# Blocks of 16 for the triangular inverse, and low weight parts kept in DRAM

## The chip, the cores and the metric

The kernel runs on one core of one Trainium2 chip. The metric is the device time in microseconds of one launch. One core has five engines that run their own instruction streams in order: TensorE (PE, with its weight loads shown as PEld), VectorE (DVE), ScalarE (ACT), GpSimd (POOL) and SyncE (SP). In this kernel every DMA is issued from SP's queue.

## The reference

One layer of a hybrid recurrent trunk: a norm, one wide projection, four recurrent mixers over four heads of 64 each, gates, an output projection and a final norm. 1024 prompt tokens are one sequence; 8 further rows are single steps of 8 sequences with carried states.

```python
h = rms_norm(x, norm_g)
proj = jnp.matmul(h, w_in)            # split among the four mixers and their gates
# gated delta rule (GDN), chunks of 64 tokens:
low  = jnp.where(strict, einsum('nbhid,nbhjd->nbhij', kb, k) * decay, 0.0)
sol  = triangular_solve(low + eye, [vb, kb * exp(gc)], lower=True, unit_diagonal=True)
# RWKV-7: s = s*exp(w) - (s @ kk) (kk*a)^T + v k^T, one token after the other
mixed = concatenate([o_gla, o_s5, o_gdn, o_rwkv])
x = x + mixed @ w_out;  y = rms_norm(x, final_g)
```

Both the delta rule and RWKV-7 are computed here in chunks of 64 tokens, and each chunk of each head needs the inverse of a unit triangular 64x64 matrix.

## The kernel before, in words

The tokens are worked through in two halves of 512 (the second one carries the 8 further rows too, so 520 columns). In each half the four mixers work on two pairs of heads each.

**Streams.** A projection of 128 output columns is `stream` (L270): its 1024x128 weights come in two chunks of 256 KB, and each chunk goes through `wsplit` (L261). SP loads it raw (`wr`, 3 buffers, L263), ACT rounds it to the high part (`wh`, 2 buffers, L266), and POOL subtracts that from the raw one for the low part (`wl`, 2 buffers, L267). PE then does three matmuls for each block of 128 rows: high weights by high inputs, high by low, low by high (L278). There are 30 projections and 8 output streams in a half, so 38 streams and 76 chunks; both halves load and split the same weights. The streams of `w_out` come last in each half (`out_stream`, L1273); those of the second half end the kernel (`tail`).

**Inverses.** `inverse` (L288) is called by each unit of RWKV and GDN: 2 mixers x 2 pairs x 2 halves = 8 times, for 16 matrices of 64x64 each. The diagonal blocks of 32x32 are gathered through DRAM so that each of 128 partitions holds one block row set (L298 writes `d1`, L301 reads it back as `LT`). VectorE eliminates them in 31 steps of two instructions: a product into `DP` (L308) and a sum into `DT` (L310). The result goes out to DRAM (`d2`, L313) and comes back into `XT` (L315). VectorE transposes (L319), and two rounds of small matmuls on PE (L324, L327), each with an ACT copy behind it, join the blocks of 32 to 64. The chunk recurrence of the unit reads `XT`.

**Order.** A unit is a generator in four stages: its projections, its preparation (stage 1, which ends with the matrix `Gt` or `Gg`), the inverse (stage 2), the recurrence (stage 3). `ORDER` (L33) lists the tokens that advance the units; R, D, L, S, g, W stand for RWKV, GDN, GLA, S5, a gate and the weights of S5, an accent for the second half. `PRI` (L32) brings a stage forward by so many instructions; R2 and D2 are the inverses. From these a scheduler fixes the order of instructions on each engine at build time, so a change in lengths moves instructions everywhere. `late` holds an instruction behind another one without a semaphore.

## Time and profile before

| | us |
|---|---|
| runs | 1046.91, 1058.57, 1059.12 (median 1058.57) |
| profiled execution | 1059.9 |
| its span, first to last instruction | 1058.1 |

| engine | busy us | share | instructions |
|---|---|---|---|
| PE | 929.8 | 88% | 5994 |
| PEld | 764.5 | 72% | 5994 |
| DVE | 698.9 | 66% | 1843 |
| ACT | 462.4 | 44% | 1088 |
| POOL | 391.1 | 37% | 439 |

The mean granted clock of TensorE is 0.854 of full. Busy time of PE is a union of modelled durations that overlap, so two matmuls that start 0.12 us apart and last 0.28 us each count as one stretch; a PE that is busy may still be far from its rate. A float32 matmul shows as two records, so 16 of them in the program are 32 in a count. The first half's own work lies in the span from about 0 to 440 us, the second half's from about 440 on, with the first half's output streams moved in between its recurrences.

### The profile page before, as it was taken

The page shows a single profiled execution, that of the slowest core. Times are in us where ns is not written, and L with a number is a line of the kernel's source. Part 1 is how long each engine was busy: PE and PEld are TensorE (multiplying, and loading weights), DVE is VectorE, ACT ScalarE, POOL GpSimd, SP SyncE. Part 2 cuts the span into 40 slices and gives each one's busy share as a digit, 9 for nine tenths or more (in the row PEclk, how much of TensorE's full clock was granted, in tenths as well). Part 3 has the DMA queues.
Part 4 walks back from the last instruction along what each step waited for, and adds up shares of the span by engine and source line. Part 5 has one row for each costly group of instructions (what it writes and reads, how often), then busy time and mean ns, then how long its engine had stood idle before and what let it go on. Part 6 is the DMA issues. An engine that isn't in the chain of part 4 may idle for free. (4 is left out here: it accounts for less than half of the span.)

```text
span 1058.1 us, 17042 instructions
## 1 busy us (share of the span) xinstructions
PE 929.8 (88%) x5994; PEld 764.5 (72%) x5994; DVE 698.9 (66%) x1843; ACT 462.4 (44%) x1088; POOL 391.1 (37%) x439
## 2 busy tenths in 40 slices
PE   3898989899998898797999989898998989897595
PEld 2676757678777686687788868777886968685594
DVE  8627895767548645836577979888976555725523
ACT  4355625331643423531663544554343354257233
POOL 2698654530221540015344513205523711432132
PEclk9999989975886866598999989868986969899697
DMA  7142423220220203125123332313121244437322
GB/s 234 56 143 77 137 74 81 80 60 5 77 63 28 81 29 120 58 64 160 50 81 96 100 91 80 92 27 85 33 62 40 83 132 132 147 117 240 139 80 91
DMA packets 85109, 95.91 MB, mean 91 GB/s; under 512 B 41640, under 2 KB 52016, under 8 KB 85024
## 3 DMA queue, kind: packets, MB, share of 16 engines
q1 hardware_dynamic: 85024, 94.83, 29.4%
q8 instruction: 47, 0.77, 0.3%
q14 instruction: 38, 0.31, 0.1%
HBM read 75.95 MB, written 16.72 MB: 88 GB/s over the span
## 5 line engine op out<-in xcount | busy, mean ns | idle before, releaser
L267 POOL TENSOR_TENSOR wl<-wr,wh 128x512 fp32r<-128x512 f32 x152 | 207.4, 1366 | 430.8 <-ACT wh L266 376.4
L278 PE MATMUL psp<-xhi,wh 128*128 128x260 f32 (+2 forms) x728 | 263.1, 362 | 4.8 <-DVE rx L357 2.2
L278 PE MATMUL psp<-xhi,wl 128*128 128x260 f32 (+2 forms) x728 | 254.0, 352 | 7.1 <-POOL wl L267 6.9
L278 PE MATMUL psp<-xlo,wh 128*128 128x260 f32 (+2 forms) x728 | 252.7, 348 | 0.7 <-DVE xlo L258 0.7
L278 PEld LDWEIGHTS psp<-xhi,wh 128*128 128x128 f32 x728 | 152.5, 209 | 26.4 <-issue 7.0
L278 PEld LDWEIGHTS psp<-xhi,wl 128*128 128x128 f32 x728 | 150.9, 208 | 26.3 <-POOL wl L267 10.9
L278 PEld LDWEIGHTS psp<-xlo,wh 128*128 128x128 f32 x728 | 152.6, 210 | 16.6 <-issue 4.4
L266 ACT CAST wh<-wr 128x512 fp32r<-128x512 f32 x152 | 93.6, 617 | 142.0 <-PE psp L278 73.5
L308 DVE TENSOR_TENSOR DP<-DT,LT 128x60 f32<-128x60 f32 (+24 forms) x248 | 76.2, 307 | 11.5 <-DMA LT<-d 5.5
L310 DVE TENSOR_TENSOR DT<-DT,DP 128x60 f32<-128x60 f32 (+24 forms) x248 | 77.0, 311 | 6.2
L278 PE MATMUL psp<-olo,wh 128*128 128x260 f32 (+1 forms) x192 | 64.5, 336 | 5.1 <-DVE olo L117 4.8
L278 PE MATMUL psp<-ohi,wh 128*128 128x260 f32 (+1 forms) x192 | 65.8, 345 | 3.4 <-ACT wh L266 1.9
L278 PE MATMUL psp<-ohi,wl 128*128 128x260 f32 (+1 forms) x192 | 63.8, 339 | 0.1
L278 PEld LDWEIGHTS psp<-olo,wh 128*128 128x128 f32 x192 | 38.3, 199 | 8.8 <-DVE olo L117 5.5
L278 PEld LDWEIGHTS psp<-ohi,wh 128*128 128x128 f32 x192 | 38.2, 200 | 6.9 <-ACT wh L266 2.3
L113 ACT ACTIVATE eg<-eg 128x260 f32<-128x260 f32 (+1 forms) x72 | 33.8, 485 | 18.7 <-DVE eg L200 18.2
L485 PE MATMUL psc<-UV,Gt 64*128 64x64 f32 (+1 forms) x256 | 39.8, 292 | 2.1 <-ACT UV L478 2.1
L278 PEld LDWEIGHTS psp<-ohi,wl 128*128 128x128 f32 x192 | 37.6, 198 | 3.0 <-POOL wl L267 0.4
L485 PEld LDWEIGHTS psc<-UV,Gt 64*128 64x128 f32 (+1 forms) x256 | 30.3, 189 | 11.5 <-issue 2.9
L117 POOL TENSOR_TENSOR df<-cum 128x256 f32<-128x256 f32 x48 | 30.4, 654 | 19.7 <-DVE cum L739 12.5
L764 PE MATMUL psb<-W 64*128 64x64 f32 x256 | 34.8, 319 | 0.1
L256 PE MATMUL psb<-constA,xn 128*128 128x128 f32 (+1 forms) x72 | 15.8, 375 | 20.3 <-DVE xn L252 9.9
(432 smaller groups left out, 1875.0 us busy)
## 6 DMA issues: line engine op xcount, KB each, us to landing
wr<-in_wct SPq DMA_DIRECT2D x120, 256.0 KB
wr<-in_wo SPq DMA_DIRECT2D x32, 256.0 KB
xn<-in_x SPq DMA_DIRECT2D x8, 512.0 KB
LT<-d SPq DMA_DIRECT2D x32, 128.0 KB
dgp<-gp SPq DMA_DIRECT2D x8, 256.0 KB
Gml<-dG SPq DMA_DIRECT2D x4, 512.0 KB
csT<-dph SPq DMA_DIRECT2D x4, 512.0 KB
dTl<-dT SPq DMA_DIRECT2D x4, 512.0 KB
```

Source lines behind the costliest of these rows:

```text
L113: A.activation(out, in_, func, bias=bias, scale=scale, **kw)
L117: return (G if ENG[name] == "G" else V).tensor_tensor(out, a, b, op)
L256: PE.transpose(pt[:, k, :n], xn[:n, (4 * b + k) * 128:(4 * b + k + 1) * 128], ident[:n, :n])
L266: A.copy(hi, raw)
L267: G.tensor_tensor(lo, raw, hi, ALU.subtract)
L278: X["mm"] = PE.matmul(p[:, :m], w[:, k % 4, :], x[:, k, c0:c0 + m], start=(i == 0 and s == 0), stop=(i == 7 and s == 2))
L308: V.tensor_tensor(tp[:, :m, :w], DT[:, :m, j:j + 1].to_broadcast([128, m, w]), LT[:, j:j + 1, j + 1:32].to_broadcast([128, m, w]), ALU.mult)
L310: V.tensor_tensor(DT[:, :m, j + 1:32], DT[:, :m, j + 1:32], tp[:, :m, :w], ALU.add)
L485: PE.matmul(o, l, r, start=start, stop=True, skip_group_check=True)
L764: PE.matmul(pg[:, c, :], W[HS[e], t], W[HS[e], t].rearrange("p (b f s) -> p f b s", f=2, s=s)[:, 1], start=True, stop=True)
```

## The change

The inverse works on diagonal blocks of 16, so VectorE has 15 steps of two instructions (30, not 62), on tiles half as wide. The gather through DRAM has one DMA for each block of 16 (twice as many), the read back two DMAs for four, the way out two for four, the way into `XT` eight for four. A round is added that joins 16 to 32: four more transposes on VectorE, 32 matmuls of 32x16, an ACT copy into `P16` (which takes the one buffer of `DP`), 32 matmuls of 16x16, four ACT copies. The two old rounds alternate between the pairs now. The zeros in `XT` are written whole by one POOL instruction.

The low part of a weight chunk is computed once: in the first half SP writes it to DRAM behind POOL's subtraction, in the second half SP loads it instead. 76 subtractions of POOL are gone, 76 stores and 76 loads of 256 KB are added, all in SP's queue. `ORDER` and `PRI` are other ones.

```diff
-PRI = {"R2": 4000, "D2": 2000, "R3": 4000, "D3": 2000, "L1": 1600, "R1": 600, "L0": 100, "L2": 600, "D0": 300, "D1": 1000}
+PRI = {"R2": 1875, "D2": 1000, "R3": 4000, "D3": 2000, "L1": 1600, "R1": 600, "L0": 100, "L2": 600, "D0": 150, "D1": 1250}
-ORDER = ("x W W t W W m R0 g6 R0 D0 W W M D0 D1 R1 W R0 R1 L0 R1 R0 L0 R1 D1 L0 g0 D0 D0 S g0 L1 g4 g6 D1 g3 g7 L1 D1 g2 L1 x' "
...
+ORDER = ("x W W t R0 m D0 W W g6 R0 W W W M D0 D1 R1 R0 R1 L0 R1 R0 L0 R1 D1 L0 g0 S g0 L1 D0 D0 g4 g6 D1 g3 g7 g2 L1 L1 D1 x' "
...
     def wsplit(src, key):
...
         A.copy(hi, raw)
-        G.tensor_tensor(lo, raw, hi, ALU.subtract)
+        if key in kept:
+            SP.dma_start(out=lo.bitcast(F32), in_=kept[key])
+        else:
+            G.tensor_tensor(lo, raw, hi, ALU.subtract)
+            kept[key] = drp.tile([128, 4, 128], F32, name=f"wk{len(kept)}")
+            SP.dma_start(out=kept[key], in_=lo.bitcast(F32))
...
     def inverse(Ga, XT, after):
...
+            for u in range(2):
+                r = slice(32 * f + 16 * u, 32 * f + 16 * u + 16)
+                for b, g in enumerate(Ga[p]):
+                    SP.dma_start(out=d1[p, f, u, nb * b:nb * b + nb].rearrange("(c e) s t -> s c e t", e=2), in_=g[r, :, :, r])
...
-        for j in range(31):
-            m = j // 4 + 1
-            w = 31 - j
+        for j in range(15):
+            m = j // 2 + 1
+            w = 15 - j
...
             V.tensor_tensor(tp[:, :m, :w], DT[:, :m, j:j + 1].to_broadcast([128, m, w]),
-                            LT[:, j:j + 1, j + 1:32].to_broadcast([128, m, w]), ALU.mult)
-            V.tensor_tensor(DT[:, :m, j + 1:32], DT[:, :m, j + 1:32], tp[:, :m, :w], ALU.add)
+                            LT[:, j:j + 1, j + 1:16].to_broadcast([128, m, w]), ALU.mult)
+            V.tensor_tensor(DT[:, :m, j + 1:16], DT[:, :m, j + 1:16], tp[:, :m, :w], ALU.add)
...
+        P16 = tmp.tile([128, 8, 16], F32, tag="DP", bufs=NB["DP"], name="P16")
+        for p, f in Q:
+            V.transpose(D16[at(p, f)], XT[at(p, f), :, 32 * f:32 * f + 32])
+        for k in range(8):
+            for p, f in Q:
+                PE.matmul(pq[at(p, f), k, 0:16], gat(p, f, k, 32 * f, 32 * f + 32), D16[at(p, f), k, 0:16], start=True, stop=True)
+        A.copy(P16, pq[:, :, 0:16])
+        for k in range(8):
+            for p, f in Q:
+                PE.matmul(pq[at(p, f, 0, 16), k, 16:32], P16[at(p, f), k, :], XT[at(p, f), k, 32 * f + 16:32 * f + 32], start=True, stop=True)
+        for p, f in Q:
+            A.copy(XT[at(p, f, 0, 16), :, 32 * f + 16:32 * f + 32], pq[at(p, f, 0, 16), :, 16:32])
```

Three places show how the order moved. In these rows a trailing xN is so many of the same in a row, and line numbers of the changed kernel are some 30 higher in the units.

On SP, the second half's first inverse (RWKV, pair 0), from the read back of the blocks to the way into `XT`. Before:

```order
L298 DMA d_5070<-Gt 32x4x32 x4
L263 DMA wr<-in_wct 128x512
L301 DMA LT<-d_5070 32x1024 x4
L263 DMA wr<-in_wct 128x512 x3
L461 DMA out_rwkv_s<-S_5230 128x512
L263 DMA wr<-in_wct 128x512
L235 DMA onst<-so 8x1x64 x2
L263 DMA wr<-in_wct 128x512 x4
L313 DMA d_5179<-DT 256x1x32 x4
L263 DMA wr<-in_wct 128x512
L315 DMA XT<-d_5179 32x8x32 x4
```

Now (L271 loads a low part, L266 a raw chunk, L324 and L327 are the ways out and back of the inverse):

```order
L266 DMA wr<-in_wct 128x512
L491 DMA out_rwkv_s<-S_5234 128x512
L271 DMA wl<-wk_713 128x512
L266 DMA wr<-in_wct 128x512
L271 DMA wl<-wk_721 128x512
L266 DMA wr<-in_wct 128x512
L235 DMA onst<-so 8x1x64 x2
L324 DMA d_5108<-DT 512x1x16 x2
L271 DMA wl<-wk_757 128x512
L327 DMA XT<-d_5108 16x8x16 x8
L266 DMA wr<-in_wct 128x512 x2
L271 DMA wl<-wk_765 128x512
```

Each raw load has a load of a low part ahead of it now, and one of these (wk_757) stands between the inverse's way out and its way back.

On VectorE, the first half's last inverse (GDN, pair 1), which is mixed with two recurrences (`state_121` is RWKV's, `state_111` GLA's; `r` and `UV` are what an RWKV chunk hands to PE). Before:

```order
L310 TENSOR_TENSOR DT<-DT,DP 128x4x19
L501 SCALAR_TENSOR_TENSOR state_121<-psc,fx,state_121 64x64 x2
L308 TENSOR_TENSOR DP<-DT,LT 128x4x18
L310 TENSOR_TENSOR DT<-DT,DP 128x4x18
L308 TENSOR_TENSOR DP<-DT,LT 128x4x17
L310 TENSOR_TENSOR DT<-DT,DP 128x4x17
L829 SCALAR_TENSOR_TENSOR state_111<-state_111,at,psc 64x64 x2
L308 TENSOR_TENSOR DP<-DT,LT 128x4x16
L123 COPY r<-psc 64x128
L310 TENSOR_TENSOR DT<-DT,DP 128x4x16
L308 TENSOR_TENSOR DP<-DT,LT 128x5x15
L829 SCALAR_TENSOR_TENSOR state_111<-state_111,at,psc 64x64 x2
```

Now (L319 and L321 are the product and the sum, L531, L859 and L123 the recurrences):

```order
L531 SCALAR_TENSOR_TENSOR state_121<-psc,fx,state_121 64x64 x2
L319 TENSOR_TENSOR DP<-DT,LT 128x15
L859 SCALAR_TENSOR_TENSOR state_111<-state_111,at,psc 64x64 x2
L123 COPY r<-psc 64x128
L321 TENSOR_TENSOR DT<-DT,DP 128x15
L319 TENSOR_TENSOR DP<-DT,LT 128x14
L859 SCALAR_TENSOR_TENSOR state_111<-state_111,at,psc 64x64
L321 TENSOR_TENSOR DT<-DT,DP 128x14
L123 COPY UV<-psc 64x128
L859 SCALAR_TENSOR_TENSOR state_111<-state_111,at,psc 64x64
L712 TENSOR_TENSOR Kn<-psc,kdn 128x128
L714 TENSOR_TENSOR Rv<-psc,ben 128x128
```

Before, up to four instructions of the inverse stand between two of the recurrences; now it is one or two, and they are narrower.

On PE, the end of the first inverse's joins. Before (L324 and L327 are the two rounds, L278 streams):

```order
L278 MATMUL psp<-xlo,wh 128x512
L485 MATMUL psc<-r,XT 64x64 x2
L324 MATMUL psi<-Dn,Gt 32x32 x8
L278 MATMUL psp<-xhi,wl 128x512
L278 MATMUL psp<-xhi,wh 128x512
L278 MATMUL psp<-xlo,wh 128x512
L442 MATMUL psb<-AR,BK 128x128 x8
L278 MATMUL psp<-xhi,wl 128x512
L485 MATMUL psc<-UV,Bn 128x128
L485 MATMUL psc<-UV,Gt 64x64 x2
L327 MATMUL psi<-XT,Dn 32x32 x8
```

Now the start of the added round (L338; L286 are streams):

```order
L286 MATMUL psp<-xhi,wh 128x512
L286 MATMUL psp<-xlo,wh 128x512
L338 MATMUL psi<-D_1608,Gt 32x16
L515 MATMUL psc<-UV,Gt 128x64 x2
L338 MATMUL psi<-D_1608,Gt 32x16 x2
L286 MATMUL psp<-xhi,wl 128x512
L286 MATMUL psp<-xhi,wh 128x512
L286 MATMUL psp<-xlo,wh 128x512
L286 MATMUL psp<-xhi,wl 128x512
L338 MATMUL psi<-D_1608,Gt 32x16 x29
L443 MATMUL psb<-ta,constB 128x512
L286 MATMUL psp<-xhi,wh 128x512
```

A round is cut into pieces that stand between stream matmuls, since the pieces for each quarter wait for their own transposes.

## Rows read from the trace of the kernel before

**Rows 1.** The page, part 1: busy time and share of the span, x instructions.
```profile
PE 929.8 (88%) x5994; PEld 764.5 (72%) x5994; DVE 698.9 (66%) x1843; ACT 462.4 (44%) x1088; POOL 391.1 (37%) x439
```

**Rows 2.** Windows: length, busy us of each engine (x count), TensorE clock, DMA share, GB/s.
```profile
120.00:160.00 40.00, 34.86 (x172) 24.94 (x170) 36.80 (x81) 16.97 (x34) 23.04 (x23) 0.91 0.35 100
160.00:320.00 160.00, 151.50 (x922) 115.73 (x922) 101.76 (x262) 65.89 (x149) 50.79 (x55) 0.82 0.22 60
320.00:360.00 40.00, 32.74 (x146) 25.76 (x145) 35.26 (x122) 15.04 (x35) 8.18 (x10) 0.67 0.14 43
560.00:800.00 240.00, 220.80 (x1696) 188.05 (x1694) 206.38 (x557) 107.33 (x255) 80.08 (x90) 0.88 0.26 73
```

**Rows 3.** Windows of tile DP alone: length, VectorE busy us (x count), clock, DMA.
```profile
120.00:160.00 40.00, 25.41 (x62) 0.91 0.35 100
160.00:320.00 160.00, 37.88 (x129) 0.82 0.22 60
320.00:360.00 40.00, 15.57 (x58) 0.67 0.14 43
560.00:800.00 240.00, 74.33 (x248) 0.88 0.26 73
```

**Rows 4.** Groups of VectorE lines: names, shapes, xcount | busy us, mean ns | idle before.
```profile
L308 DVE TENSOR_TENSOR DP<-DT,LT 128x60 f32<-128x60 f32 (+24 forms) x248 | 76.2, 307 | 11.5 <-DMA LT<-d 5.5
L310 DVE TENSOR_TENSOR DT<-DT,DP 128x60 f32<-128x60 f32 (+24 forms) x248 | 77.0, 311 | 6.2
L319 DVE STREAM_TRANSPOSE Dn<-XT 32x256 f32<-32x256 f32 x16 | 6.9, 433 | 7.4 <-DMA XT<-d 7.1
...
L310 DVE TENSOR_TENSOR DT<-DT,DP 128x28 f32<-128x28 f32 x16 | 8.6, 539 | 0.3
L310 DVE TENSOR_TENSOR DT<-DT,DP 128x29 f32<-128x29 f32 x8 | 1.7, 207 | 0.3
```

**Rows 5.** Line 267: ns min/median/max, first and last start.
```profile
L267 POOL TENSOR_TENSOR wl<-wr,wh x152: 1253/1285/2583, 16.7 to 1038.9; 128x512 fp32r<-128x512 f32 x152
```

**Rows 6.** Timeline of PE, from 364 us: start, us, instruction, xcount.
```profile
364.17 0.40 PE L278 MATMUL psp<-xhi,wh 128*128 128x512 f32 x1
364.40 0.40 PE L278 MATMUL psp<-xlo,wh 128*128 128x512 f32 x1
364.73 0.69 PE L324 MATMUL psi<-Dn,Gg 32*32 32x32 f32 x16
365.34 0.68 PE L761 MATMUL psb<-W 64*64 64x64 f32 x8
```

**Rows 7.** Timeline of SP's queue, first inverse: start, us, issues.
```profile
111.28 1.76 SPq L298 DMA_DIRECT2D d<-Gt  x4
...
159.56 2.55 SPq L313 DMA_DIRECT2D d<-DT  x4
...
163.63 2.08 SPq L315 DMA_DIRECT2D XT<-d  x4
```

**Rows 8.** Timeline: a weight load issued, and the cast that waits for its landing.
```profile
925.75 0.40 SPq L263 DMA_DIRECT2D wr<-in_wo  x1
...
928.14 0.62 ACT L266 CAST wh<-wr 128x512 fp32r<-128x512 f32 x1 [1.41 <-DMA wr<-in_wo]
```

**Rows 9.** Timeline of the last streams: a cast, and the subtraction behind it.
```profile
1012.25 0.62 ACT L266 CAST wh<-wr 128x512 fp32r<-128x512 f32 x1 [0.74 <-PE psp L278]
...
1012.95 1.29 POOL L267 TENSOR_TENSOR wl<-wr,wh 128x512 fp32r<-128x512 f32 x1 [1.34 <-ACT wh L266]
```

**Rows 10.** Waits: who <- for whom: us in total, times, longest.
```profile
SPq L263 <- POOL wl L267: 361.4, 95, 18.9
SPq L298 <- DVE Gg L655: 38.6, 3, 19.8
...
PE psp L278 <- POOL wl L267: 6.9, 7, 2.9
```

More of the change, by code (lines that the diff above doesn't have):

```diff
@@ L266, in wsplit, with stream @@
         A.copy(hi, raw)
-        G.tensor_tensor(lo, raw, hi, ALU.subtract)
+        if key in kept:
[4 more added lines that the diff above has]
+            SP.dma_start(out=kept[key], in_=lo.bitcast(F32))
         return hi, lo
-    def stream(wsrc, evac, order=range(8)):
-        wt = {q: wsplit(wsrc[:, 4 * q:4 * q + 4, :]) for q in dict.fromkeys(k // 4 for k in order)}
+    def stream(wsrc, key, evac, order=range(8)):
+        wt = {q: wsplit(wsrc[:, 4 * q:4 * q + 4, :], (key, q)) for q in dict.fromkeys(k // 4 for k in order)}
         for c0, m in X["pieces"] or pieces(X["n"]):
@@ L281, in proj @@
     def proj(ct, evac):
-        stream(I["wct"][ct], evac)
+        stream(I["wct"][ct], ct, evac)
     def prt(name):
@@ L291, in inverse @@
         Q = [(p, f) for p in range(2) for f in range(2)]
[L292 to L293 removed]
+        at = lambda p, f, u=0, n=32: slice(64 * p + 32 * f + 16 * u, 64 * p + 32 * f + 16 * u + n)
+        nb = 8 // len(Ga[0])
+        d1 = drp.tile([2, 2, 2, 8, 16, 16], F32, tag="d1", bufs=NB["d1"], name="d1")
         for p, f in Q:
[L295 to L298 removed]
@@ new lines, in inverse @@
+        LT = tmp.tile([128, 16, 16], F32, tag="LT", bufs=NB["LT"], name="LT")
+        for q in range(2):
+            SP.dma_start(out=LT[64 * q:64 * q + 64], in_=d1.rearrange("p f u x s t -> (p f u x) s t"))
+        DT = tmp.tile([128, 8, 16], F32, tag="DT", bufs=NB["DT"], name="DT")
+        late(SP.dma_start(out=DT.rearrange("p m i -> p (m i)"), in_=I["dinit"]), after)
+        late(G.memset(XT, 0.0), after)
+        for j in range(15):
+            m = j // 2 + 1
+            w = 15 - j
+            tp = tmp.tile([128, 8, 16], F32, tag="DP", bufs=NB["DP"], name="DP")
+            V.tensor_tensor(tp[:, :m, :w], DT[:, :m, j:j + 1].to_broadcast([128, m, w]),
+                            LT[:, j:j + 1, j + 1:16].to_broadcast([128, m, w]), ALU.mult)
+            V.tensor_tensor(DT[:, :m, j + 1:16], DT[:, :m, j + 1:16], tp[:, :m, :w], ALU.add)
@@ new lines, in inverse @@
+        d2 = drp.tile([2, 2, 2, 8, 16, 16], F32, tag="d2", bufs=NB["d2"], name="d2")
+        for q in range(2):
+            SP.dma_start(out=d2.rearrange("p f u x (m q) i -> q (p f u x) m i", q=2)[q], in_=DT[64 * q:64 * q + 64])
+        for p, f in Q:
+            for u in range(2):
+                SP.dma_start(out=XT[at(p, f, u, 16), :, 32 * f + 16 * u:32 * f + 16 * u + 16], in_=d2[p, f, u].rearrange("x c i -> c x i"))
+        gat = lambda p, f, k, t0, t1: Ga[p][k // nb][32 * f:32 * f + 32, k % nb // 2, k % 2, t0:t1]
@@ L319, in inverse @@
             V.transpose(Dn[at(p, 0)], XT[at(p, 0), :, 0:32])
-        pi = ps_i.tile([128, 2, 8, 32], F32, tag="i", name="psi")
-        pq, po = pi[:, 0], pi[:, 1]
+        for k in range(8):
+            for p in range(2):
+                PE.matmul(po[at(p, 1), k, :], gat(p, 0, k, 32, 64), Dn[at(p, 0), k, :], start=True, stop=True)
         for p in range(2):
-            for k in range(8):
-                PE.matmul(pq[at(p, 1), k, :], Ga[p][k // nb][0:32, k % nb // 2, k % 2, 32:64], Dn[at(p, 0), k, :], start=True, stop=True)
-            A.copy(Dn[at(p, 1)], pq[at(p, 1)])
-            for k in range(8):
+            A.copy(Dn[at(p, 1)], po[at(p, 1)])
@@ L327, in inverse @@
+        for k in range(8):
+            for p in range(2):
                 PE.matmul(po[at(p, 0), k, :], Dn[at(p, 1), k, :], XT[at(p, 1), k, 32:64], start=True, stop=True)
+        for p in range(2):
             A.copy(XT[at(p, 0), :, 32:64], po[at(p, 0)])
@@ L1278, in evac @@
             A.copy(yT[:, c0:c0 + k], p)
-        stream(I["wo"][m], evac, [2 * b + p for b, p in GORD])
+        stream(I["wo"][m], ("o", m), evac, [2 * b + p for b, p in GORD])
         pt = psc(128, 4, 128)
```

32 lines of the change are left out of this document (10 added, 22 removed).

## The prediction

> **What bounds the kernel now.** First the busy shares [rows 1]: PE is busy 88% of the span, VectorE 66%, POOL 37%. PE looks like the bound, but its busy time is no measure of its rate, so I went to the windows by stage and read the clock beside the busy times [rows 2]. The reader is to see three stretches, 120 to 160, 320 to 360 and 560 to 800 us, where VectorE is busy 36.80 of 40, 35.26 of 40 and 206.38 of 240, together 278.4 of 320 us (87%), while the TensorE clock is 0.91, 0.67 and 0.88 of full. [...] There VectorE sets the pace: PE, in order, waits for the small copies of the chunk recurrences, and these stand behind the inverses. The windows of tile DP alone [rows 3] give the inverses' part: 25.4 + 15.6 + 74.3 = 115.3 us of VectorE in the three stretches, and 37.9 us more between 160 and 320, where VectorE is 64% busy. Elsewhere there is no inverse.
>
> **The inverse's two-instruction loop.** A step's instructions have means of 307 and 311 ns [rows 4], with 62 an inverse 19.2 us, 153.2 in all. The forms of 28 and of 29 elements have 539 and 207 ns: size isn't what counts, collisions are. Undisturbed, the narrower ones should take no more than that 207 ns; with some collisions left I take 220 ns, between 207 and 309. So 30 instructions take 6.6 us, 0.345 of before (0.32 to 0.48 at those ends). Of the 115.3 us, 39.7 stay and 75.6 go. The added round brings four transposes an inverse at 433 ns [rows 4], for the six inverses or so of these stretches 10.4 us. Net 65 us of VectorE. At an unchanged share of 87% that shortens the stretches by 65 / 0.87 = 75 us. [...] Between 160 and 320 the same factor frees 24.8 us less 3.5 of transposes, 21; with VectorE 64% busy I take half, 11 us, ends 0 and 21.
>
> **The way through DRAM.** The gathers have 8 DMAs more for an RWKV inverse and 4 for a GDN one, at 1.76 / 4 = 0.44 us of SP each; the way back has 4 more at 2.08 / 4 = 0.52; the way out has 2 fewer at 2.55 / 4 = 0.64, the read back 2 fewer at about the gather's price [rows 7]. That is 6 x 0.44 + 2.1 - 1.3 - 0.9 = 2.5 us later on average, on the path of each inverse, and SP is past it that much later for the loads behind. The added round comes to some 4 us more (four transposes at 0.43, and 2.5 us of joins, below). The loop is 12.6 us shorter, so an inverse is still ready some 6 us earlier. [...] `P16` sits in the one buffer of `DP`, so a following inverse can't start its loop before the added round of the one before is read. Where two follow each other closely, some of the gain goes there; I price it at nothing, as the loop that waits is so much shorter, at some 6 us three times if that cover is gone. The POOL instruction for the zeros and ACT's five copies an inverse lie beside other work: both engines are busy under half of the time [rows 1].
>
> **The added joins on PE.** 64 matmuls an inverse are 128 records. Sixteen of the old ones, twice as wide, took 365.34 - 364.73 = 0.61 us, 38 ns each [rows 6]. By that the round costs 4.9 us an inverse, 39 us in all; at half the width, and with quarters that follow one another, it may be a quarter of it. I take half, 20 us, of which 12 fall where PE is the one waited for; ends 2 and 39. [...]
>
> **The low parts.** 76 POOL instructions of 1285 ns [rows 5], 98 us, leave the second half. POOL isn't the bound there (80 of 240 us [rows 2]), so this gains only what VectorE no longer waits behind POOL. The collisions in the inverses are 496 x (309 - 207) ns = 51 us at most; of the rest of VectorE's work in the second half I take 5 us, ends 0 and 30.
>
> The 76 stores stand behind POOL's subtraction in SP's queue, but raw loads already waited there for POOL, 361.4 us in 95 waits [rows 10], without PE feeling it (6.9 us). I cost them at nothing: a landing of about 2.4 us [rows 8] is over before the chunk's 12 matmuls of 512 columns at 0.23 us are [rows 6], so `wl` comes free for POOL's next subtraction as before. Without that cover it is at most 10 us.
>
> The 76 loads are another matter. Before, the raw chunk waited in one of three buffers, and from a free buffer to a finished low part was a cast and a subtraction, from 1012.25 to 1014.24, 2.0 us [rows 9]. Now SP may issue the load only when the buffer is free, and a load took 2.39 us from issue to the cast behind its landing [rows 8]; a raw load just ahead makes it later. Where streams follow each other this is 0.4 us or more a chunk. PE's recurrence work stands between most streams and hides it; at 0.2 us for each of 38 streams I take 8 us, ends -5 and 90 (2.4 us each).
>
> **Order.** The new `ORDER` and `PRI` can't be priced from this trace: 0, with 10 us either way.
>
> **Sum.** -45 - 11 + 12 - 5 + 8 = -41 on the profiled execution's 1059.9 us, which stands 1.3 us above the median of the runs. That is 1019 us. What is late next is PE: the streams, and the chains of the recurrences.
>
> **Rivals.** *Low parts come too late (slower).* SP is in order, and the load of a low part stands behind the inverses' DMAs: in the second half one stands between way out and way back, and SP waited up to 19.8 us for a `Gg` [rows 10]. Three raw buffers covered this before; nothing covers the low part now. PE then waits at the streams, and its clock falls. At 2 us for each of the 38 streams of the second half this is 76 us in place of 8: 1087 us. It decides from 1.8 us a stream, where the sum passes 1080. Against it: SP's long waits were few, three for `Gg`, and the order puts the loads well ahead of some streams. Chance 0.10.
>
> *VectorE wasn't the limit.* The chains PE to VectorE to PE and the landing times stay, and PE keeps its 88%; then the 45 and 11 don't come, and 1059.9 + 12 - 5 + 8 is 1075, or near 1055 with a few us of them. For it: PE was idle only 32 of the 320 us. Against it: the clock. Chance 0.25.
>
> *The collisions go too (much faster).* A VectorE instruction that collides waits for the whole of POOL's: 28 elements took 539 ns on average against 207 for 29. If the 98 us of POOL that go blocked VectorE for a third of their time in the second half, 30 us go in place of 5, and the time is 994. For it: the 51 us within the inverses alone. Against it: POOL's other work stays. [...] Chance 0.15.
>
> That the change doesn't do what it says is no rival: the order has 76 stores and 76 loads of low parts, and 30 instructions an inverse.
>
> **Numbers.** The likeliest case, 0.50, is 1019 us, in itself 990 to 1045. The range, 980 to 1070, takes in it, the third rival and most of the second. About 2% (1037 to 1080) is what a measurement of this kernel can tell from no change. Faster: 0.46 of the likeliest and 0.15, with 0.03 of the second rival, 0.64. Same: 0.04 and 0.22, 0.26. Slower: 0.10.
>
> **What would show it.** In the changed profile the loop's lines should hold 45 to 60 us, VectorE 580 to 610 in all, POOL near 290, with 76 subtractions. In the stretches of the inverses the clock should be nearer to 1 and PE's waits for `r`, `UV` and `U` shorter. The last eight streams, 1000 to 1045 us before, should take as long as they did, and PE's waits for `wl` stay under 15 us. The forecast is wrong if PE waits for loads of `wl` by some us at many streams, if the clock stays at 0.85 with VectorE idle, or if the added rounds take over 5 us of PE an inverse.

## The result, and the profile after

The changed kernel takes 1041.1 us in the median of four runs (1035.7 to 1045.8), against 1058.7 before: a ratio of 0.985, with a 95% interval of 0.980 to 0.990, some 16 us less. The prediction was 41 us less. The ratios and intervals here are of each kernel's faster runs, of which e2 below has two, of 1075.9 and 1086.7 us, and four slower ones, of 1092.5 to 1097.0, one of them in its trace. The profiled execution took 1045.8 us, with a span of 1043.7.

The first line of the page, busy times and shares, answers to [rows 1]:

```profile
PE 931.7 (89%) x7018; PEld 759.9 (73%) x7018; DVE 604.4 (58%) x1619; ACT 474.7 (45%) x1128; POOL 290.2 (28%) x355
```

VectorE lost 94.5 us and POOL 101 us, about as forecast, and the span only 14. So the work went away; the time did not follow it. The groups of the loop, of the low parts and of POOL's subtractions, by line, answer to [rows 4, 5]:

```profile
L319 DVE TENSOR_TENSOR DP<-DT,LT 128x30 f32<-128x30 f32 (+10 forms) x120 | 31.6, 263 | 7.9 <-DMA LT<-d 4.9 <-issue 0.3
L321 DVE TENSOR_TENSOR DT<-DT,DP 128x30 f32<-128x30 f32 (+10 forms) x120 | 30.2, 252 | 3.0
...
L273 POOL TENSOR_TENSOR wl<-wr,wh 128x512 fp32r<-128x512 f32 x76 | 101.2, 1333 | 186.1 <-ACT wh L269 153.5 <-PE psp L286 13.3 <-ACT UV L507 7.5
```

The loop holds 61.8 us in place of 153.2. Now the windows of [rows 2], at the same times (the first inverse begins some 18 us later here, so the first row is less its own stretch than the others):

```profile
core 0: us, PE busy (x) PEld busy (x) DVE busy (x) ACT busy (x) POOL busy (x), PEclk, DMA share, GB/s
120.00:160.00 40.00, 29.42 (x149) 19.54 (x149) 34.56 (x63) 20.49 (x39) 25.04 (x22) 0.77 0.36 107
160.00:320.00 160.00, 151.58 (x1315) 113.82 (x1313) 91.01 (x210) 70.01 (x164) 49.66 (x53) 0.86 0.31 88
320.00:360.00 40.00, 34.62 (x179) 26.70 (x177) 27.58 (x95) 16.19 (x35) 8.05 (x7) 0.83 0.30 82
560.00:800.00 240.00, 228.83 (x2258) 194.12 (x2257) 163.13 (x459) 118.10 (x286) 41.85 (x64) 0.91 0.36 101
```

VectorE is busy 225.3 of 320 us (70%) where it was 87%. PE, however, stands idle 27 us there where it stood 32. The clock records of the two traces, 56 before and 52 now, are all 0.50 or 1.00 of full (before, windows of 1 us read 0.50 each from 379 to 408 us, and the stretch from 310 to 318 reads 1.00), so a mean clock c stands for 2 x (1 - c) of its stretch at the lower one. By [rows 2] that was 2 x (0.09 x 40 + 0.33 x 40 + 0.12 x 240) = 91 us, and it is still 2 x (0.23 x 40 + 0.17 x 40 + 0.09 x 240) = 75. By these windows, which don't hold quite the same work before and after, little of PE's idle time or of its time at the lower clock has gone. Over the whole span PE's idle time went from 128 to 112 us and the time at the lower clock, by the trace's clock records, from 308 to 264, while PE had the added round to do. PE's waits, before and then after, have changed little (line that waits, what for, us in total, times, longest):

```profile
PE psc L691 <- DVE U L123: 7.2, 9, 1.6
PE psc L485 <- DVE UV L123: 6.5, 9, 1.6
...
PE psc L691 <- DVE r L695: 2.1, 4, 1.1
```

```profile
PE psc L721 <- DVE U L123: 8.4, 8, 3.2
...
PE psp L286 <- POOL wl L273: 5.7, 6, 3.3
...
PE psp L286 <- DMA wl<-wk: 4.4, 6, 1.2
...
PE psc L721 <- DVE r L725: 3.8, 6, 1.2
...
PE psc L515 <- DVE UV L123: 1.5, 3, 0.7
```

For `U`, `UV` and `r` PE waited 15.8 us before and 13.7 now. The other side grew: VectorE's wait for PE before `r` (line 725, 695 before) went from 14.8 to 22.9 us. All of VectorE's waits for PE's `psc` went from 140 to 172 us. So VectorE, with less to do, waits more for PE.

### The profile page after: what moved, and what is told of

It reads as the page before. It is cut to its first block, busy times and chain, and to the rows that moved or that the text cites. A ratio compares the mean times of both kernels' runs of the same rounds, so it can differ in the third digit from the quotient of the medians.

```text
span 1043.7 us, 19159 instructions
## 1 busy us (share of the span) xinstructions
PE 931.7 (89%) x7018; PEld 759.9 (73%) x7018; DVE 604.4 (58%) x1619; ACT 474.7 (45%) x1128; POOL 290.2 (28%) x355
## 4 chain that ended last, share of the span: by engine, by line
PE 64%; DVE 16%; DMA 7%; ACT 6%; issue 3%; POOL 3%; SPq 2%; ACTq 0%; DVEq 0%; POOLq 0%
PE psp L286 35%; PE psc L515 5%; PE psc L721 3%; PE psb L794 3%; DMA wl<-wk 2%; PE psb L815 1%; PE psc L851 1%; POOL wl L273 1%; DVE DT L321 1%; PE psb L472 1%; PE psb L227 1%; DVE DP L319 1%; DMA constB<-in_constB 1%; PE psb L1180 1%; PE psb L1181 1%
## 5 line engine op out<-in xcount | busy, mean ns | idle before, releaser
L286 PE MATMUL psp<-xhi,wl 128*128 128x260 f32 (+2 forms) x728 | 251.7, 349 | 8.6 <-POOL wl L273 5.7
L286 PE MATMUL psp<-xhi,wh 128*128 128x260 f32 (+2 forms) x728 | 255.4, 351 | 4.0 <-DVE gp L1250 1.9
L286 PE MATMUL psp<-xlo,wh 128*128 128x260 f32 (+2 forms) x728 | 247.4, 340 | 0.9 <-DVE xlo L258 0.9
L286 PEld LDWEIGHTS psp<-xhi,wl 128*128 128x128 f32 x728 | 146.4, 202 | 29.7 <-POOL wl L273 8.5
L286 PEld LDWEIGHTS psp<-xhi,wh 128*128 128x128 f32 x728 | 147.8, 203 | 26.3 <-issue 6.5
L286 PEld LDWEIGHTS psp<-xlo,wh 128*128 128x128 f32 x728 | 147.8, 203 | 15.0 <-issue 2.7
L273 POOL TENSOR_TENSOR wl<-wr,wh 128x512 fp32r<-128x512 f32 x76 | 101.2, 1333 | 186.1 <-ACT wh L269 153.5
L286 PE MATMUL psp<-olo,wh 128*128 128x260 f32 (+1 forms) x192 | 65.2, 340 | 6.5 <-DVE olo L117 6.1
L286 PE MATMUL psp<-ohi,wh 128*128 128x260 f32 (+1 forms) x192 | 65.7, 346 | 4.8 <-ACT ohi L1299 4.7
L286 PE MATMUL psp<-ohi,wl 128*128 128x260 f32 (+1 forms) x192 | 64.3, 341 | 1.8 <-DMA wl<-wk 1.8
L286 PEld LDWEIGHTS psp<-olo,wh 128*128 128x128 f32 x192 | 38.6, 201 | 10.7 <-DVE olo L117 7.5
L286 PEld LDWEIGHTS psp<-ohi,wh 128*128 128x128 f32 x192 | 37.9, 199 | 8.2 <-ACT ohi L1299 5.5
L286 PEld LDWEIGHTS psp<-ohi,wl 128*128 128x128 f32 x192 | 38.1, 201 | 4.8 <-DMA wl<-wk 2.2
L515 PE MATMUL psc<-UV,Gt 64*64 64x64 f32 (+1 forms) x256 | 38.8, 282 | 2.7 <-ACT UV L508 1.4
L113 ACT ACTIVATE eg<-eg 128x260 f32<-128x260 f32 (+1 forms) x72 | 33.3, 484 | 16.2 <-DVE eg L200 15.5
L515 PEld LDWEIGHTS psc<-UV,Gt 64*64 64x64 f32 (+1 forms) x256 | 29.6, 182 | 11.4 <-issue 4.8
L319 DVE TENSOR_TENSOR DP<-DT,LT 128x30 f32<-128x30 f32 (+10 forms) x120 | 31.6, 263 | 7.9 <-DMA LT<-d 4.9
L794 PEld LDWEIGHTS psb<-W 64*128 64x128 f32 x256 | 31.7, 226 | 3.1 <-issue 0.9
```

Source lines behind the costliest of these rows:

```text
L113: A.activation(out, in_, func, bias=bias, scale=scale, **kw)
L273: G.tensor_tensor(lo, raw, hi, ALU.subtract)
L286: X["mm"] = PE.matmul(p[:, :m], w[:, k % 4, :], x[:, k, c0:c0 + m], start=(i == 0 and s == 0), stop=(i == 7 and s == 2))
L319: V.tensor_tensor(tp[:, :m, :w], DT[:, :m, j:j + 1].to_broadcast([128, m, w]), LT[:, j:j + 1, j + 1:16].to_broadcast([128, m, w]), ALU.mult)
L515: PE.matmul(o, l, r, start=start, stop=True, skip_group_check=True)
L794: PE.matmul(pg[:, c, :], W[HS[e], t], W[HS[e], t].rearrange("p (b f s) -> p f b s", f=2, s=s)[:, 1], start=True, stop=True)
```

## Experiments

All were timed beside the kernel before. Two kinds are used. In the first, parts of the change are put in or left out in the source, and the scheduler orders the program anew. In the second ("order kept"), instructions are altered after the scheduler has finished: every engine has its list of instructions, waits and signals unchanged, and only what some of them do is smaller (e6 adds copies instead, and e17 and e18 also drop 76 waits). Only the second kind measures a cost by itself, as the first four runs made plain.

### The parts, each with an order of its own

e1 puts only the blocks of 16 into the kernel before:

```diff
-        for j in range(31):
-            m = j // 4 + 1
+        for j in range(15):
+            m = j // 2 + 1
...
+                PE.matmul(pq[at(p, f), k, 0:16], gat(p, f, k, 32 * f, 32 * f + 32), D16[at(p, f), k, 0:16], start=True, stop=True)
```

> The blocks of 16 alone, with the old order tables and every low part subtracted on POOL in both halves. Theory A (VectorE set the pace, as forecast): -45 - 11 + 12 = -44 us, about 1015 us, with the inverse loop near 60 us. Theory B (VectorE's freed time turns into VectorE idle time, since PE and the chains of the recurrences set the pace): between 1045 and 1065 us, VectorE's busy time some 85 us less, PE's idle time nearly unchanged. Theory C (the gain was there and the kept low parts or the new order took it back): as A, 1015 to 1025.

e2 puts in only the kept low parts:

```diff
-        G.tensor_tensor(lo, raw, hi, ALU.subtract)
+        if key in kept:
+            SP.dma_start(out=lo.bitcast(F32), in_=kept[key])
+        else:
...
```

> The kept low parts alone, with blocks of 32 and the old order tables. As forecast: -5 + 8 = +3 us, 1050 to 1070, POOL near 295 us busy. Theory C (loads of low parts that come late took the gain back): 1075 us or more, with PE waiting for loads of wl by 0.5 us or more at many of the 38 streams of the second half, and the last eight streams some 10 us longer. Theory B: within 1% of before.

e3 only the two tables:

```diff
-PRI = {"R2": 4000, "D2": 2000, "R3": 4000, "D3": 2000, "L1": 1600, "R1": 600, "L0": 100, "L2": 600, "D0": 300, "D1": 1000}
-ORDER = ("x W W t W W m R0 g6 R0 D0 W W M D0 D1 R1 W R0 R1 L0 R1 R0 L0 R1 D1 L0 g0 D0 D0 S g0 L1 g4 g6 D1 g3 g7 L1 D1 g2 L1 x' "
+PRI = {"R2": 1875, "D2": 1000, "R3": 4000, "D3": 2000, "L1": 1600, "R1": 600, "L0": 100, "L2": 600, "D0": 150, "D1": 1250}
+ORDER = ("x W W t R0 m D0 W W g6 R0 W W W M D0 D1 R1 R0 R1 L0 R1 R0 L0 R1 D1 L0 g0 S g0 L1 D0 D0 g4 g6 D1 g3 g7 g2 L1 L1 D1 x' "
...
```

> The new ORDER and PRI alone. As forecast: within 10 us of 1059. Theory B makes the order the thing that moves the time: 10 to 20 us either way; the first RWKV inverse starts some 18 us later as it does in the changed kernel. Theory C: slower by 15 us or more.

e4 is e1 and e2 together, so the change without e3's edit:

```diff
+        for j in range(15):
...
+        if key in kept:
...
```

> Blocks of 16 and kept low parts with the old order tables: the change without its third part. If the parts add up, this is e1 and e2 together. Theory A: about 1018 us. Theory B: 1040 to 1062, and the changed kernel's 17 us come in good part from the order tables. Theory C by the order: about 1020, clearly faster than the changed kernel's 1041.

e7 is the changed kernel without e2's edit, e8 without e1's:

```diff
-        if key in kept:
-            SP.dma_start(out=lo.bitcast(F32), in_=kept[key])
...
```

> The changed kernel without the kept low parts: blocks of 16 and the new order tables. Theory C (late low parts took the gain back): 1010 to 1030 us. As forecast for that part (-5 + 8): 1038, within 1% of the changed kernel. Theory E (the order tables fit one set of costs only, and any part taken out moves the scheduler's order): slower than the changed kernel by 10 us or more, whatever part is taken out.

```diff
-        for j in range(15):
+        for j in range(31):
...
```

> The changed kernel with the old blocks of 32: kept low parts and the new order tables. Theory A: about 1041 + 44 = 1085 us. Theory B: 1045 to 1060. Theory E: over 1051, and since e2 alone cost 25 us and e3 alone 49, anything up to 1110.

Ratios to the kernel before, with 95% intervals:

| low parts | old tables, blocks of 32 | old tables, blocks of 16 | new tables, blocks of 32 | new tables, blocks of 16 |
|---|---|---|---|---|
| subtracted in both halves | 1 | e1: 1.001 (0.998 to 1.005) | e3: 1.046 (1.041 to 1.051) | e7: 1.039 (1.034 to 1.043) |
| kept | e2: 1.024 (1.015 to 1.032) | e4: 0.996 (0.992 to 1.000) | e8: 0.997 (0.993 to 1.001) | the change: 0.985 (0.980 to 0.990) |

The parts don't add up. e3 has the instructions of the kernel before, in another order, and takes 49 us longer. The same swap of tables costs 40 us with blocks of 16 and saves 28 and 11 with kept low parts. e2 looks like theory C by its time, but not by its signs: PE waits for loads of `wl` 9.7 us in 13 places, 1.8 at the longest, and the stretch from the last wait for `olo` to the end is 2 us longer, not 10. e7, where the loads are gone and the time is longer, gives theory C no support either, but its order is another one too; e17 below prices the loads at a kept order. So any edit that makes the scheduler order anew is measured together with an order worth up to 49 us: theory E, and no part can be priced from this table alone. It does show that the blocks of 16 bring less than theory A's -4.2% under each of these orders: +0.1%, -2.7%, -0.7% and -1.2%.

In e3's worse order PE has more time without a matmul of a stream. By the start times of the stream's line (278 or 286), stretches of over 3 us without one come to 346 us before, 414 in e3, 339 in the changed kernel. Windows of the longest two of e3:

```profile
389.00:452.00 63.00, 54.31 (x301) 45.35 (x301) 43.32 (x120) 27.14 (x69) 12.61 (x17) 0.57 0.14 46
878.00:920.00 42.00, 38.67 (x202) 30.66 (x200) 26.26 (x78) 16.49 (x46) 7.93 (x9) 0.63 0.22 71
```

PE is busy 93 of these 105 us, with small matmuls of the recurrences at a granted clock of 0.57 and 0.63, and no other engine is near its limit.

e15 and e16 are the changed kernel with the first half of the old order list, with the new and with the old `PRI`:

```diff
-ORDER = ("x W W t R0 m D0 W W g6 R0 W W W M D0 D1 R1 R0 R1 L0 R1 R0 L0 R1 D1 L0 g0 S g0 L1 D0 D0 g4 g6 D1 g3 g7 g2 L1 L1 D1 x' "
+ORDER = ("x W W t W W m R0 g6 R0 D0 W W M D0 D1 R1 W R0 R1 L0 R1 R0 L0 R1 D1 L0 g0 D0 D0 S g0 L1 g4 g6 D1 g3 g7 L1 D1 g2 L1 x' "
...
```

> The changed kernel with the order list of before up to t' and the new one behind it; PRI new. By the recurrences' own times the first half ended 5 us earlier under the old list (first RWKV step of the second half at 606 us against 611), the second half is 10 us shorter under the new one (433 against 443): if the halves are independent, about 1036 us. If the scheduler's choices in one half hang on the other, anything from 1030 to 1090.

```diff
-PRI = {"R2": 1875, "D2": 1000, "R3": 4000, "D3": 2000, "L1": 1600, "R1": 600, "L0": 100, "L2": 600, "D0": 150, "D1": 1250}
+PRI = {"R2": 4000, "D2": 2000, "R3": 4000, "D3": 2000, "L1": 1600, "R1": 600, "L0": 100, "L2": 600, "D0": 300, "D1": 1000}
...
```

> As e15 with the PRI of before. If the halves are independent: about 1036; else between 1040 and 1090. e15 and e16 differ in three PRI values only (R2, D2, D0, D1 of the inverses' and chunks' stages), so their distance is what such numbers are worth.

e15: 0.999 (0.996 to 1.001), e16: 0.993 (0.989 to 0.996). Neither beats the change, and the halves are not independent. (The expectation says three values of `PRI` and names four; four differ.)

### What the loop is worth at an unchanged order

e5 cuts each of the loop's 496 instructions to one element a partition:

```diff
+one = lambda a: PhysicalAccessPattern(ap=[list(a.ap[0]), [1, 1]], offset=a.offset, ...)
+for i, x in enumerate(b.instructions):      # after the scheduler
+    if uses(x, "DP_"):
+        b.instructions[i] = copy.replace(x, ins=[one(a) for a in x.ins], outs=[one(a) for a in x.outs])
```

> The kernel before with its order of instructions kept on every engine; the 496 instructions of the inverses' loop work on one element a partition (the inverses come out wrong). It asks what VectorE's time in the loop is worth when nothing else moves. At some 100 ns an instruction VectorE loses about 100 us. Theory A (VectorE sets the pace; the scheduler's new order gave it back in e1): 1000 to 1025 us, with the clock above 0.9 in the stretches of the inverses. Theory B (freed VectorE time turns into VectorE idle time, as PE's order and the recurrences set the pace): 1040 to 1060.

0.981 (0.975 to 0.987), 21 us less. But VectorE was not freed of 100 us, only of 28, since an instruction of one element still took 262 and 249 ns on average, where the loop's full sizes took 307 and 311 (groups by line):

```profile
L308 DVE TENSOR_TENSOR DP<-DT,LT 128x1 f32<-128x1 f32 x248 | 64.9, 262 | 11.5 <-DMA LT<-d 5.5
L310 DVE TENSOR_TENSOR DT<-DT,DP 128x1 f32<-128x1 f32 x248 | 61.8, 249 | 6.2
```

So e5 fits neither theory as I had put it: three quarters of it came off in time, for a small piece. e9 takes the rest away, by memsets that read nothing:

```diff
+for i, x in enumerate(b.instructions):      # after the scheduler
+    if uses(x, "DP_"):
+        b.instructions[i] = InstMemset(name=x.name, outs=[one(x.outs[0])], sync_info=x.sync_info, ...)
```

> The kernel before with its order, waits and signals kept on every engine; the loop's 496 instructions become one-element memsets, which were 59 ns elsewhere in this kernel and read nothing, so that they need not stand behind POOL (the inverses come out wrong). VectorE loses some 115 us of 153. e5 freed only 28 us of VectorE and 20 us (14 to 27) of the time came off. Theory A (VectorE sets the pace in the stretches of the inverses, as forecast: 0.6 to 0.7 us of time for each of its us): 975 to 1000 us. Theory B (a little of VectorE's time is on the path, then PE's own order and chains take over): 1025 to 1040, no faster than e5 by more than 10 us.

0.958 (0.955 to 0.962), 44 us less, for 107.8 us of VectorE (698.9 before): 0.41 us for each.

```profile
PE 902.8 (89%) x5994; PEld 744.5 (73%) x5994; DVE 591.1 (58%) x1843; ACT 462.8 (46%) x1088; POOL 394.0 (39%) x439
```

This lies between the theories: VectorE was on the path, at well under the 0.69 (45 of 65) of the forecast, and the whole loop is worth less than the forecast had for two thirds of it.

e12 does the same in the changed kernel, whose loop is already short:

```diff
+    if uses(x, "DP_"):
+        b.instructions[i] = InstMemset(name=x.name, outs=[one(x.outs[0])], sync_info=x.sync_info, ...)
```

> The changed kernel with its order, waits and signals kept; the loop's 240 instructions become one-element memsets (the inverses come out wrong). VectorE loses some 45 of its 62 us there. Theory A: another 20 to 30 us, 1011 to 1021. Theory B: 1033 to 1042.

0.977 (0.973 to 0.981), so 9 us (2 to 15) below the changed kernel for 39.6 us of VectorE: 0.2 us for each, less than e9's 0.41. That is theory B's range, in an order that is not e9's.

```profile
PE 935.3 (90%) x7018; PEld 765.0 (74%) x7018; DVE 564.8 (54%) x1619; ACT 474.8 (46%) x1128; POOL 288.6 (28%) x355
```

### POOL's subtractions at an unchanged order

e10 turns the 76 subtractions of the second half into memsets of 0.53 us; e11 is e9 and e10 in one:

```diff
+    if x.name in second_half_lows:
+        b.instructions[i] = InstMemset(name=x.name, outs=x.outs, sync_info=x.sync_info, ...)
```

> The kernel before with its order, waits and signals kept; the second half's 76 subtractions of low parts on POOL become memsets of the same tile (the low parts are left out there, so the output is less exact). It prices POOL's time and its collisions with VectorE in the second half, without loads or stores. As forecast: -5 us, ends 0 and -30. Theory F (collisions are worth much more): -30 us. Theory B: within 5 us of before.

```diff
+    if x.name in second_half_lows or uses(x, "DP_"):
+        b.instructions[i] = InstMemset(...)
```

> e9 and e10 in one kernel. If VectorE sets the pace: 970 to 995 us. If the two parts are separate, the sum of both; theory B: 1020 to 1035.

e10: 0.980 (0.976 to 0.984), 21 us less, four times the forecast's 5 and under theory F's 30. The page has the likeliest reason:

```profile
PE 916.5 (89%) x5994; PEld 756.4 (73%) x5994; DVE 662.9 (64%) x1843; ACT 462.5 (45%) x1088; POOL 326.8 (32%) x439
```

No VectorE instruction was altered, and VectorE is busy 36 us less. The trace before shows where such time lies: at 567.40 us a sum of the loop started 0.06 us behind a subtraction of the second half, took 1.30 us and ended 0.07 us behind it, while the product of the same size at 566.67, with POOL idle, took 0.21:

```profile
566.67 0.21 DVE L308 TENSOR_TENSOR DP<-DT,LT 128x50 f32<-128x50 f32 x1
...
567.34 1.29 POOL L267 TENSOR_TENSOR wl<-wr,wh 128x512 fp32r<-128x512 f32 x1 [2.29 <-ACT wh L266]
567.40 1.30 DVE L310 TENSOR_TENSOR DT<-DT,DP 128x50 f32<-128x50 f32 x1
```

PE's own waits for POOL's `wl` are no part of the gain: 6.9 us before, 6.7 in e10. e11, however, is 0.955 (0.951 to 0.958), only 4 us below e9: with the loop gone, hardly any of what e10 frees is waited for.

### What the change frees, at an unchanged order

e13 leaves an inverse's first 15 steps at the width of a block of 16, with `j // 4 + 1` in place of `j // 2 + 1` rows of it, so with as many elements or down to half, and turns the other 16 into memsets. e14 has e10's edit on top:

```diff
+    if uses(x, "DP_"):
+        j = seen[tile] // 2
+        b.instructions[i] = memset(x) if j >= 15 else cut(x, m=min(j // 2 + 1, j // 4 + 1), w=15 - j)
```

> The kernel before with its order, waits and signals kept; of an inverse's 31 steps the first 15 keep the sizes of a block of 16, the other 16 become one-element memsets of 59 ns (the inverses come out wrong). This is what the change takes from the loop, without its added transposes, joins, DMAs and without a new order. On the line through e5 (28 us of VectorE freed, 20 of time) and e9 (108 freed, 44 of time), some 80 us freed should bring 34 to 38 us: 1018 to 1026. The forecast's -45 - 11, with the 13.9 us of transposes put back, asks for about -65: 993. If it is below 25 us, the loop's first steps matter more than its last.

```diff
+    if x.name in second_half_lows:
+        b.instructions[i] = memset(x)
```

> e13 with the second half's 76 POOL subtractions as memsets too: all that the change frees, at the old order and with none of its costs. The forecast's -45 - 11 - 5: 998. From e9 to e11 the second part brought 4 us on top: 1014 to 1024. If it is 1010 or less, the parts add up better while some of the loop is left.

e13: 0.980 (0.975 to 0.985), 21 us less, with VectorE busy 637.9, so for 61 us of it. The line through e5 and e9 had asked for 34 to 38. By the expectation's own words a gain below 25 means that the loop's first steps matter more than its last; no run tests that by itself. Its page, and its windows of the same PE work as 120 to 160, 160 to 320, 320 to 360 and 560 to 800 before (PE's order is the same in both kernels, and the counts of its matmuls agree with [rows 2] to within one):

```profile
PE 917.3 (88%) x5994; PEld 756.8 (73%) x5994; DVE 637.9 (61%) x1843; ACT 462.6 (44%) x1088; POOL 392.2 (38%) x439
```

```profile
120.60:158.20 37.60, 34.59 (x172) 25.03 (x170) 30.60 (x81) 18.88 (x37) 23.74 (x23) 0.91 0.39 106
158.20:313.00 154.80, 148.23 (x921) 113.41 (x920) 85.25 (x265) 63.77 (x145) 49.75 (x54) 0.83 0.23 62
313.00:348.40 35.40, 30.86 (x147) 24.30 (x146) 28.03 (x119) 15.04 (x35) 8.15 (x10) 0.71 0.16 49
544.70:781.80 237.10, 220.54 (x1696) 189.45 (x1694) 176.97 (x561) 107.50 (x255) 81.18 (x90) 0.87 0.27 73
```

The three stretches take 310 us. Between the starts of the same matmuls it was 321 before (120.2 to 160.1, 320.0 to 360.3, 560.2 to 801.0). The stretch between the first and the second takes 155 us and took 160.

e14: 0.967 (0.963 to 0.971), 35 us less. Its page, and the three stretches by the same PE work:

```profile
PE 910.6 (89%) x5994; PEld 755.0 (73%) x5994; DVE 612.9 (60%) x1843; ACT 462.0 (45%) x1088; POOL 329.1 (32%) x439
```

```profile
119.60:158.20 38.60, 34.70 (x172) 24.91 (x170) 29.89 (x81) 19.11 (x38) 24.08 (x24) 0.91 0.37 105
312.20:347.50 35.30, 29.85 (x146) 23.82 (x145) 28.29 (x121) 14.90 (x34) 7.74 (x10) 0.76 0.17 49
546.60:775.70 229.10, 218.39 (x1697) 188.02 (x1695) 159.06 (x561) 107.20 (x255) 52.01 (x90) 0.88 0.28 76
```

With 86 us of VectorE gone and nothing added, they take 303 us. PE's idle time in them fell from 32 to 20 us, and the lower clock held 2 x (0.09 x 38.6 + 0.24 x 35.3 + 0.12 x 229.1) = 79 us, against 91. In e9, with 108 us gone, the same work takes 290 us, 16 of them idle and 57 at the lower clock:

```profile
120.50:152.80 32.30, 31.85 (x171) 22.96 (x170) 20.34 (x81) 18.90 (x38) 24.98 (x24) 1.00 0.45 126
302.80:334.60 31.80, 26.77 (x146) 20.71 (x145) 23.80 (x111) 14.97 (x34) 7.91 (x10) 0.89 0.18 54
534.60:760.50 225.90, 215.59 (x1696) 184.64 (x1694) 155.10 (x561) 107.60 (x255) 81.14 (x90) 0.89 0.28 77
```

One trace is a rough guide to the clock, as the executions of the kernel before beside e13 and e14 differ in it from 0.849 to 0.874. Averaged over the runs behind the ratios, 2 x (1 - clock) x span is 300 us before, 268 in e13 and 252 in e14, and 237 in e9 against 296 before. In the trace before, a stream's matmuls of 512 columns start 0.43 us apart at the lower clock (306.5 to 309.4 us, clock 0.50) and 0.23 at the full one (310 to 318 us, clock 1.00). If all of PE's work goes like that, some half of each difference, 16, 24 and 30 us, is what the faster clock gave, an estimate: the larger part of the 21, 35 and 44 us that came off. So PE's idle time and its time at the lower clock do shrink when VectorE is freed, but only in part.

Much of what stays lies in stretches without a stream. Before, 191 of the 308 us at the lower clock fall into the 346 us counted above; in e14 it is 164 of 265, in 325 us. Three of these stretches before, and the same work in e14:

```profile
379.00:405.00 26.00, 24.32 (x132) 20.60 (x131) 14.14 (x35) 7.68 (x18) 5.37 (x6) 0.50 0.04 11
413.00:447.00 34.00, 25.46 (x127) 19.69 (x126) 25.36 (x76) 17.75 (x44) 3.45 (x4) 0.59 0.19 64
685.00:706.00 21.00, 18.44 (x80) 13.44 (x80) 16.96 (x58) 15.60 (x38) 3.81 (x3) 0.58 0.17 46
```

```profile
366.00:388.00 22.00, 20.31 (x130) 17.46 (x130) 14.68 (x35) 7.51 (x18) 5.74 (x6) 0.61 0.04 13
396.00:431.00 35.00, 25.91 (x128) 19.89 (x127) 26.33 (x79) 18.81 (x47) 3.44 (x4) 0.58 0.22 71
664.00:684.00 20.00, 18.00 (x80) 13.02 (x79) 14.97 (x57) 15.49 (x37) 2.78 (x3) 0.59 0.20 48
```

The reader is to see PE busy 68.2 of 81 us before and 64.2 of 77 after, at a clock of 0.5 to 0.6 both times. These stretches are chains of small matmuls with short VectorE steps between them. Only the last of the three lies in the forecast's stretches and has instructions of the loop in it (6.4 us of VectorE before, 4.5 in e14); in all they are 4 us shorter. In the forecast's own three stretches 54 of the 91 us at the lower clock fall where no stream runs. Whether PE's fixed order or the chains of the recurrences hold the rest back, no run separates.

### What the change adds

e6 runs 431 of the added round's 512 matmuls twice in the changed kernel (those that neither wait nor signal):

```diff
+for x in b.instructions:                    # after the scheduler
+    out.append(x)
+    if added_join(x) and x.sync_info is None:
+        out.append(copy.replace(x, name=nc.get_next_instruction_name()))
```

> The changed kernel with its order kept; 431 of the 512 matmuls of the added round run twice. This prices the round itself. As forecast (38 ns a record at most, half of it taken, 12 of 20 us on the path): +10 us beside the changed kernel's 1041, within +2 and +33. Theory D (the added round is what took the gain back): +25 us or more. Theory B: +0 to +10, PE some 17 us busier.

0.994 (0.991 to 0.996): 9 us (3 to 15) above the changed kernel, and by the share of all 512, 10.5 us for the round, so theory D falls. PE is busy 14.7 us more than in the changed kernel (931.7), 17.5 by that share. PE's changes between tiles of 128x128 and of 32x32 or 32x16 are not in this, as a copy follows a matmul of its own tile size.

```profile
PE 946.4 (90%) x7880; PEld 776.9 (74%) x7880; DVE 602.5 (57%) x1619; ACT 474.2 (45%) x1128; POOL 290.3 (28%) x355
```

e17 takes the loads of the low parts out of the changed kernel, e18 the stores as well:

```diff
+    if low_load(x):       # after the scheduler: 128x1, into DRAM, nobody waits
+        b.instructions[i] = copy.replace(x, outs=[small(x.ins[0])], ins=[small(const)])
+    elif reads_low(x):    # 608 matmuls; 76 waits for the loads go
+        b.instructions[i] = copy.replace(x, ins=with_low_part_of_x(x), sync_info=without_dma_waits(x))
```

> The changed kernel with its order kept; in the second half the matmuls of the low part take 128 columns of x's low part as weights and no longer wait for the load of wl; each of the 76 loads becomes a store of one element a partition that nobody waits for (the low parts are left out there). This prices the loads: their landing, their 256 KB each and PE's wait. As forecast (+8, ends -5 and 90): 1033 us. If the chain that ended last in the changed kernel (2.1% of it in these loads, 22 us) is right: 1020 to 1028. If the loads are hidden and the new order has the rest: 1037 to 1045.

```diff
+    elif low_store(x):
+        b.instructions[i] = copy.replace(x, outs=[small(x.outs[0])], ins=[small(x.ins[0])])
```

> e17, and the first half's 76 stores of low parts write one element a partition. The forecast has the stores at 0 (at most 10 us): as e17, within 1%. If their 256 KB each hold up other transfers of the first half: 5 to 10 us less than e17.

e17: 0.977 (0.972 to 0.983), 9 us (1 to 16) below the changed kernel. e18: 0.976 (0.971 to 0.981), 1 us below e17, not to be told from it. The loads cost what the forecast had, the stores nothing that shows. The chain that ended last in the changed kernel had overstated the loads, at 2% or 22 us:

```profile
PE psp L286 35%; PE psc L515 5%; PE psc L721 3%; PE psb L794 3%; DMA wl<-wk 2%; PE psb L815 1%; PE psc L851 1%; POOL wl L273 1%; DVE DT L321 1%; PE psb L472 1%; PE psb L227 1%; DVE DP L319 1%; DMA constB<-in_constB 1%; PE psb L1180 1%; PE psb L1181 1%
```

## Why the prediction was wrong

**The failing step is the sum's 45 us, and with it the 11.** The forecast turned 65 us of VectorE in the three stretches into 45 of time and 21 more into 11. The 45 was the author's estimate and no run shows it: in e13's trace the three stretches are 11 us shorter, and the one between is 5, not 11. e13 frees VectorE of most of what the change takes from the loop, in the kernel before at an unchanged order and without the added transposes that the forecast had taken off: 61 us of VectorE go, 21 us of time come off (16 to 26), not 56. That is 0.35 us for each, where the forecast had 0.65 (56 for 86). e13 keeps 256 memsets of 59 ns (15 us) that the change doesn't have; at the slope from e13 to e9, 23 us of time for 47 of VectorE, they would be worth some 7 us more, an estimate, which still leaves half of the 56.

The direction was right: by the runs' clocks some 16 of e13's 21 us came with a faster clock (the estimate above), and PE's idle time over the span fell by 6 us in its trace. The forecast read the low clock of the three stretches as PE waiting for VectorE. Of the 91 us at the lower clock there 54 lie where PE has no stream to run, only chains of small matmuls, and such stretches stayed slow for the most part with VectorE freed (191 us at the lower clock before, 164 in e14).

The sum, with what each term measured:

| term | forecast | measured at an unchanged order |
|---|---|---|
| loop, both terms | -56 | -21 (e13, 16 to 26) |
| POOL's subtractions, beside that | -5, ends 0 and -30 | -14 (e14 less e13, 7 to 21) |
| added joins | +12, ends 2 and 39 | +10.5 (e6) |
| loads of low parts | +8, ends -5 and 90 | +9 (e17, 1 to 16) |
| stores | 0 | 1 (e18, within 8) |
| new order, transposes, the way through DRAM, changes of PE's tile size | 0, 10 either way | not measured apart; the sum leaves about 0, by some 12 us either way |

The measured terms come to -15.5, the chip gave -16 (-10 to -21). That closes it better than their intervals allow one to claim: e13 and e14 stand in the old order, e6 and e17 in the new, and e13's memsets may hide some 7 us that the unmeasured row would then have cost. The joins and the loads were right in kind and size; that 0.2 us a stream and half a round proved right is in part luck, as their ends were wide. POOL's term was nearly three times the 5, within its ends. (e14 still has POOL's 76 memsets of 0.53 us, which the change doesn't have.) As the sign that would show it wrong the forecast had allowed the joins 5 us of PE an inverse; by e6 it is 2.2 of PE's busy time and 1.3 on the path.

**VectorE's time.** The loop was forecast at 53 us and is 61.8, 257 ns an instruction and not 220. The narrower instructions are shorter in the median, 185 ns against 218 or 220, and under the forecast's 207; e5's, with one element, take 159. What the forecast had too small is the waiting on top: it allowed 13 ns above its 207, and the mean stands 73 ns above the median in the changed kernel, 90 before and 96 in e5. So the loop has half the instructions, and each of them waits nearly as long on top (ns min/median/max of one of the loop's two lines, in the kernel before, in e5 and in the changed kernel):

```profile
L308 DVE TENSOR_TENSOR DP<-DT,LT x248: 160/218/1303, 124.6 to 766.6; 128x60 f32<-128x60 f32 x12, 128x54 f32<-128x54 f32 x8, 128x66 f32<-128x66 f32 x8, 128x28 f32<-128x28 f32 x8
```

```profile
L308 DVE TENSOR_TENSOR DP<-DT,LT x248: 106/159/1304, 125.2 to 745.1; 128x1 f32<-128x1 f32 x124
```

```profile
L319 DVE TENSOR_TENSOR DP<-DT,LT x120: 119/185/1296, 143.0 to 721.6; 128x30 f32<-128x30 f32 x24, 128x14 f32<-128x14 f32 x16, 128x24 f32<-128x24 f32 x16, 128x15 f32<-128x15 f32 x8
```

VectorE at 604 us and POOL at 290, with 76 subtractions, are as forecast.

**The low parts.** PE's waits for `wl` are 5.7 us on POOL and 4.4 on the loads, under the 15 set as a sign. The last eight streams took as long as they did. From the last wait for `olo` to the end it is 1058.1 - 993.5 = 64.6 us before and 1043.7 - 978.5 = 65.2 after (PE's timeline, before and after):

```profile
993.47 0.58 PE L278 MATMUL psp<-olo,wh 128*128 128x260 f32 x1 [4.33 <-DVE olo L117]
```

```profile
978.50 0.59 PE L286 MATMUL psp<-olo,wh 128*128 128x260 f32 x1 [4.34 <-DVE olo L117]
```

**The order.** Zero for the change as a whole is what the sum leaves, unmeasured by itself, but "10 us either way" was far too narrow a bound: the same tables are worth +49 to -28 us on its neighbours.

**The rivals.** Late low parts did not come. "VectorE wasn't the limit" is nearest in time, with 1055 for "a few us" of the 56, where 21 came. Its reason, the chains that stay, fits the stretches without a stream, but VectorE was on the path: e9 brought 44 us. "The collisions go too" is real by itself (e10, 21 us), and its gain overlaps with the loop's: 14 us beside e13, 4 beside e9. The sign of failure that the text had named, a clock that stays at 0.85 with VectorE idle, was met halfway: the clock of the whole span went from 0.854 to 0.873.
